# A hybrid retention and attention block: the row factor leaves the rotation of retention's keys and queries, and the setup is put in another order

## The chip, the cores and the metric

The kernel runs on one core of one Trainium2 chip. The metric is the device time of one execution in microseconds (us), the median over runs of the kernel. Engine names in the profile: PE is TensorE (matrix products), PEld its weight loads, DVE is VectorE, ACT is ScalarE, POOL is GpSimd, SP is SyncE, which issues most DMA transfers here.

## What is computed

One layer over T = 16 + 1024 rows of width 1024 (16 learned meta rows are put in front). All of it is float32. The reference, cut:

```python
u = _rms_norm(h, pre_w)                      # h * rsqrt(mean(h*h) + eps) * pre_w
rq, rk, rv, rg, aq, ak, av, ag, gr, ga = _split_in(u @ w_in)
rq = _pad_front(_rotary(rq.reshape(B, T, RET_HEADS, RET_DK), pos))
rk = _pad_front(_rotary(rk.reshape(B, T, RET_HEADS, RET_DK), pos) * (RET_DK ** -0.5))
o_r = _bidirectional_retention(rq, rk, rv, lg_f, lg_b)[:, META_PAD:]
o_r = (o_r - mu) * lax.rsqrt(var + EPS)      # per row and head, over 256 values
y_r = (o_r * ret_nw * silu(rg)) @ w_rb
y_a = (_windowed_sink_attention(aq, ak, av, sink) * silu(ag)) @ w_ab
out = (sigmoid(gr) * y_r + sigmoid(ga) * y_a) @ w_o
return h + _rms_norm(out, post_w)
```

Retention, for a chunk of 128 rows and one direction, is `inner = (q kT * decay) v`, `cross = (q * q_decay) S` and the state `S = chunk_decay * S + (k * k_decay)T v`. There are four heads, with 128 columns of q and k and 256 of v.

The normalization of a row is one number, r = (mean(x*x) + eps) to the power -1/2. Every projection of u is r times the projection of x * pre_w, so r can be put in late. In retention a key and its value always meet in a product, and a query stands alone in its output row: with unscaled keys and queries, v * r * r gives each key row its two factors, and the output row takes the query's r.

## The kernel before

*Products.* A float32 product is made of three fp32r products: each operand is split into a high part (hi, rounded) and the rest (lo), and `mm3` adds hi·hi, lo·hi, hi·lo (lines 70, 71 and 72 of the profile). ScalarE or GpSimd writes a hi, VectorE a lo (`dve_lo`, L78). Weights come as two raw tiles `wr` a unit and are split into `wh`, `wl` (`load_w`). The normalized input without its row factor, xT * pre_w, lies in SBUF as eight 128-row blocks (k = 0 to 7) of hi and lo, the tiles `big` (`xh[k]`, `xl[k]`).

*Setup.* For each k, ScalarE makes `xh` (L250), VectorE `xl` (L251), TensorE adds the block's part to all of head 0's q and k (`qk0_mm`, 18 products, into six PSUM banks `pq0`, `pk0`), ScalarE squares the raw block (L256). The squares are summed over k in two running sums (L260): blocks 0 to 4 on VectorE, the others (from `SQ2` = 5) on GpSimd. Then TensorE sums both over the partitions with a column of ones (L267, `pms`, plain float32), VectorE makes `ms` and GpSimd `rcol`, the row factor r with rows on partitions (L270, a power). The last block's `qk0_mm` comes after that in the text. `pv0` is the value projection of chunk 0 for head 0. `rw` and `rb` spread r over columns with TensorE, `rbc` is r along the free axis, and the rotation tables `cr` and `sr` are multiplied by it (L285, L286). After that `evac_qk0` rotates head 0's q and k out of PSUM (`rope_evac`: three VectorE products `m_qk`, L137 to L139, and one GpSimd sum, L140).

*Decays.* `decays()` makes lg, the log of the decay, from `dect` in a chain of some twenty 128x8 steps on GpSimd (L163 to L174), then `ex` (L176, L178) and with one power `dtab` (L181), the columns of decay factors. `decay_table` makes the 128x128 tables `DT` from lg: two VectorE products `dd` (L188, L189), an exponential on ScalarE, a scale on VectorE (L191).

*Retention.* For head h, `retention(h, fill)` runs `stage1(c + 1)` and `stage2(c)` over nine chunks (chunk 0 is the 16 meta rows), then a backward sweep. `stage1` makes pv (24 products; `pj`, three PSUM banks), its scaled parts `vh` (L373) and `vl` (L374), the transposed keys and the scores (`tr`, L377 and L379, bank `p1`), the decayed keys `khf`, `klf`, `khb`, `klb` (L387, L388) and the masked scores `sd`, `sh`, `sl`. `stage2` makes the outputs `pa`, evicted into `op` with `qdf` (L417, L418), and the states `pkv`, `Sf`, with their parts `Shf` (GpSimd) and `Slf`. `fill` runs a piece of the next head's q and k projections (`gen_qk`) in the backward sweep, and in the last head the first of attention's (`gen_ak`, `gen_aq`, `gen_gate`). Attention, gates and the three output products follow.

*Order.* Engines run their instructions in order. That order is not the text's: a scheduler with a time model orders the instructions of each engine when the kernel is built, so an instruction can stand well ahead of where the text has it. PSUM has eight banks: `pj` 3, `p1` 2, `p2` 2, `p3` 1; the six of the setup take two `pj`, one `p1`, both `p2` and `p3`.

## Time and profile before

| what | us |
|---|---|
| median of 3 runs | 1106.45 (1105.11 to 1109.32) |
| the profiled execution's own time | 1105.68 |
| its span, first to last instruction | 1103.9 |
| TensorE's granted clock over the span, share of full speed | 0.991 |

A row of the timeline or of a group reads: start, duration, engine, line, operation, output<-inputs with their shapes, count, and in brackets the idle time of that engine before it and what ended it. A row of waits reads: who waited, for whom, us in total, times, longest. A row of stretches reads: start:end and length in us, busy time (and instructions) of TensorE, its weight loads, VectorE, ScalarE and GpSimd, then TensorE's mean granted clock as a share of full speed, the share of the DMA engines in use and GB/s. Durations of instructions that follow one another closely overlap a little, so from start to start is what an instruction costs in a row of others.

### The profile page before, as it was taken

The page shows a single profiled execution, that of the slowest core. Times are in us where ns is not written, and L with a number is a line of the kernel's source. Part 1 is how long each engine was busy: PE and PEld are TensorE (multiplying, and loading weights), DVE is VectorE, ACT ScalarE, POOL GpSimd, SP SyncE. Part 2 cuts the span into 40 slices and gives each one's busy share as a digit, 9 for nine tenths or more (in the row PEclk, how much of TensorE's full clock was granted, in tenths as well). Part 3 has the DMA queues.
Part 4 walks back from the last instruction along what each step waited for, and adds up shares of the span by engine and source line. Part 5 has one row for each costly group of instructions (what it writes and reads, how often), then busy time and mean ns, then how long its engine had stood idle before and what let it go on. Part 6 is the DMA issues. An engine that isn't in the chain of part 4 may idle for free.

```text
span 1103.9 us, 17325 instructions
## 1 busy us (share of the span) xinstructions
PE 1077.2 (98%) x6034; PEld 929.5 (84%) x6034; DVE 863.3 (78%) x1830; ACT 486.8 (44%) x1126; POOL 255.9 (23%) x378
## 2 busy tenths in 40 slices
PE   6899999999999999999999999999999999999996
PEld 5799999999988888988888787888888788787885
DVE  5477787878976798988667876888889889867765
ACT  6132141422513544545557644445456546433442
POOL 7532433323232245455220000000000000010032
PEclk9799999999999999999999999999999999999998
DMA  7201111102114971021114753779783765789463
GB/s 285 77 1 39 58 58 39 52 26 66 52 48 134 346 245 58 21 96 39 68 48 153 257 200 109 231 242 357 264 274 125 233 205 192 236 202 332 116 115 76
DMA packets 75655, 159.45 MB, mean 144 GB/s; under 512 B 7984, under 2 KB 19760, under 8 KB 74800
## 3 DMA queue, kind: packets, MB, share of 16 engines
q1 hardware_dynamic: 72112, 152.06, 40.4%
q0 software_dynamic: 3456, 6.29, 3.9%
q8 instruction: 47, 0.77, 0.3%
q14 instruction: 40, 0.33, 0.1%
HBM read 105.89 MB, written 52.43 MB: 143 GB/s over the span
## 4 chain that ended last, share of the span: by engine, by line
PE 88%; DMA 4%; POOL 3%; ACT 2%; DVE 2%; issue 1%; SPq 1%; DVEq 0%; POOLq 0%; ACTq 0%
PE bz L70 7%; PE bz L71 6%; PE bz L72 6%; PE pv L70 3%; PE pv L72 3%; PE pv L71 3%; PE paq L71 3%; PE paq L72 3%; PE paq L70 3%; PE bo L71 2%; PE br L71 2%; PE bo L70 2%; PE bo L72 2%; PE br L70 2%; PE br L72 2%; PE ba L71 2%
## 5 line engine op out<-in xcount | busy, mean ns | idle before, releaser
L940 POOL DMA_DIRECT2D mx_d<-c1a x4 | 3.7, 920 | 398.1 <-DVE c1a L931 398.1
L71 PE MATMUL bz<-big,llz 128*128 128x512 f32 x208 | 82.5, 397 | 0.4 <-DVE llz L78 0.3
L71 PE MATMUL pv<-wh,big 128*128 128x256 f32 (+1 forms) x288 | 82.4, 286 | 0.0
L70 PE MATMUL pv<-wh,big 128*128 128x256 f32 (+1 forms) x288 | 81.8, 284 | 0.2 <-DVE vl L374 0.2
L72 PE MATMUL bz<-big,lhz 128*128 128x512 f32 x208 | 81.9, 394 | 0.0
L72 PE MATMUL pv<-wl,big 128*128 128x256 f32 (+1 forms) x288 | 81.6, 283 | 0.0
L70 PE MATMUL bz<-big,lhz 128*128 128x512 f32 x208 | 81.4, 396 | 0.2 <-ACT lhz L661 0.2
L70 PE MATMUL bz<-T,lhz 128*128 128x512 f32 x156 | 61.7, 396 | 1.7 <-ACT T L638 1.3
L71 PE MATMUL bz<-T,llz 128*128 128x512 f32 x156 | 61.5, 394 | 0.0
L78 DVE TENSOR_TENSOR wl<-wr,wh 128x1024 fp32r<-128x1024 f32 x34 | 46.4, 1365 | 19.3 <-POOL wh L75 19.2
L72 PE MATMUL bz<-T,lhz 128*128 128x512 f32 x156 | 61.3, 394 | 0.0
L1091 ACT ACTIVATE p<-p,nm 128x400 f32<-128x400 f32 (+1 forms) x64 | 38.3, 600 | 35.6 <-DVE nm L1089 32.8
L70 PEld LDWEIGHTS pv<-wh,big 128*128 128x128 f32 (+1 forms) x288 | 51.4, 179 | 1.7 <-DVE vl L374 0.9
L1102 POOL TENSOR_SCALAR p<-p,den 128x400 f32<-128x400 f32 (+1 forms) x60 | 36.1, 612 | 71.9 <-DVE den L1097 42.4
L71 PEld LDWEIGHTS pv<-wh,big 128*128 128x128 f32 (+1 forms) x288 | 51.4, 178 | 1.2
L72 PEld LDWEIGHTS pv<-wl,big 128*128 128x128 f32 (+1 forms) x288 | 51.4, 179 | 0.9
L71 PE MATMUL paq<-big,wl 128*128 128x512 f32 x128 | 51.3, 401 | 0.0
L70 PE MATMUL paq<-big,wh 128*128 128x512 f32 x128 | 51.0, 399 | 0.0
L72 PE MATMUL paq<-big,wh 128*128 128x512 f32 x128 | 50.9, 397 | 0.0
L70 PEld LDWEIGHTS bz<-big,lhz 128*128 128x128 f32 x208 | 39.1, 188 | 10.2 <-ACT lhz L661 1.1
L71 PEld LDWEIGHTS bz<-big,llz 128*128 128x128 f32 x208 | 39.1, 188 | 9.8 <-DVE llz L78 0.9
L72 PEld LDWEIGHTS bz<-big,lhz 128*128 128x128 f32 x208 | 39.1, 188 | 8.8
(593 smaller groups left out, 3636.0 us busy)
## 6 DMA issues: line engine op xcount, KB each, us to landing
wr<-in_w_in_dram SPq DMA_DIRECT2D x35, 512.0 KB, 3.6
wrz<-in_w_in_dram SPq DMA_DIRECT2D x28, 512.0 KB, 5.3
tg<-tg_d SPq DMA_DIRECT2D x32, 256.0 KB, 4.4
T<-preT SPq DMA_DIRECT2D x6, 1024.0 KB, 7.7
oTr_d<-ost SPq DMA_DIRECT2D x16, 256.0 KB, 2.1
xs<-in_xT_dram SPq DMA_DIRECT2D x16, 256.0 KB, 5.1
xsT<-xs SPq DMA_DIRECT2D x16, 256.0 KB, 5.1
oTa_d<-oa SPq DMA_DIRECT2D x16, 256.0 KB, 2.2
```

What stands on the lines that cost most here:

```text
L70: nc.tensor.matmul(o, ah, bh, start=first, stop=False, **kw)
L71: nc.tensor.matmul(o, al, bh, start=False, stop=False, **kw)
L72: nc.tensor.matmul(o, ah, bl, start=False, stop=last, **kw)
L78: nc.vector.tensor_tensor(o, i, hi.bitcast(F32), ALU.subtract)
L940: nc.gpsimd.dma_start(d, to, accum_op=ALU.add)
L1091: nc.scalar.activation(p[:, 0:wid], p[:, 0:wid], AF.Exp, scale=-1.0, bias=nm_[:, e_:e_ + 1], accum_out=den[:, e_:e_ + 1])
L1102: nc.gpsimd.tensor_scalar(pt[e_][:, 0:wid], pt[e_][:, 0:wid], den[:, e_:e_ + 1], 1.0, op0=ALU.mult, op1=ALU.mult)
```

## The change

- Head 0's q and k, and those of every head, are rotated with the plain tables. Values are scaled by `r2` = 1 / ms, which is r * r, in place of r. The output takes r of its row: the eviction of `pa` on ScalarE is scaled by `rcol`, and the factors on the cross terms are `qd` = rcol * dtab, eight small VectorE products for all heads and chunks.
- `rbc` and the tables with r are made later: `row_factors()` runs at the start of the last head, since attention and the gates still use them. The spreading products become transposes.
- All squares are summed on VectorE, in a chain (`q_ = sq + q_`). The sum is split into `sqh` (ScalarE) and `sql` (VectorE), and TensorE sums the two with fp32r ones, two columns wide.
- All eight blocks of `qk0_mm` run in the loop; the first piece of `evac_qk0` stands ahead of the sum, the others behind it. `pv0` of its own is gone.
- `ex` is made on ScalarE and in `decay_columns`; `dtab` is scaled on VectorE. `decay_table` for head h + 1 is called in head h.
- `tc.issue_after(split)` puts every instruction that its block traces on the engine of `split` (VectorE, the one that makes `sql`) behind it in that engine's order; other engines get no such edge.
- Loads: x block 0's first half and `dect` go to ScalarE's queue, ahead of and behind its first activation; `tabt` goes behind the rotation tables; `xr` has eight buffers in place of six.

In the built order of the changed kernel, VectorE's `dd` and `DT` stand behind `sql`; on ScalarE the product `ex` = lg * 128 stands right ahead of `xh` of block 5; VectorE's rotations of all six pieces of head 0 stand ahead of the first `vl`; TensorE's order behind the last `qk0_mm` is pv of chunk 0, of chunk 1, the sums `pms` (one of them inside pv of chunk 0), pv of chunk 2, transposes and the first `pkv`, then pv of chunk 3.

The diff, cut to its core:

```diff
-    def dve_lo(o, i, hi):
-        nc.vector.tensor_tensor(o, i, hi.bitcast(F32), ALU.subtract)
+        return nc.vector.tensor_tensor(o, i, hi.bitcast(F32), ALU.subtract).ins
...
-            g.tensor_scalar(ex[:, 4 * j:4 * j + 4], lg[:, base:base + 4], idx[:, j:j + 1], 1.0, op0=ALU.mult,
-                            op1=ALU.mult)
-        g.tensor_scalar(ex[:, 20:28], lg, float(P), 1.0, op0=ALU.mult, op1=ALU.mult)
-
-    def decay_columns():
+            nc.scalar.activation(ex[:, 4 * j:4 * j + 4], lg[:, base:base + 4], AF.Copy, scale=idx[:, j:j + 1])
+        nc.scalar.activation(ex[:, 20:28], lg, AF.Copy, scale=float(P))
         nc.gpsimd.tensor_tensor(dtab, ecst, ex, ALU.pow)
         for a, b in ((0, 8), (16, 20)):
-            nc.gpsimd.tensor_scalar(dtab[:, a:b], dtab[:, a:b], SCALE, 1.0, op0=ALU.mult, op1=ALU.mult)
+            nc.vector.tensor_scalar(dtab[:, a:b], dtab[:, a:b], SCALE, None, op0=ALU.mult)
...
-        nc.sync.dma_start(dect, dec.partition_broadcast(P))
-        xr = [st.tile([P, T], F32, tag="xr", bufs=6, name=f"xr{k}") for k in range(KT)]
+        xr = [st.tile([P, T], F32, tag="xr", bufs=KT, name=f"xr{k}") for k in range(KT)]
...
+        nc.scalar.dma_start(xr[0][:, 0:528], xT[0, :, 0:528])
+        nc.scalar.dma_start(dect, dec.partition_broadcast(P))
+        nc.sync.dma_start(vec, vecs)
...
-            if k < KT - 1:
-                qk0_mm(k)
-            q_ = st.tile([P, T], F32, tag="sq" if k else "sq0", bufs=4 if k else 1, name=f"sq{k}")
+            qk0_mm(k)
+            q_ = st.tile([P, T], F32, tag="sq", bufs=4, name=f"sq{k}")
             nc.scalar.activation(q_, t, AF.Square)
-            if k in (0, SQ2):
-                sq.append(q_)
-            else:
-                (nc.gpsimd if k > SQ2 else nc.vector).tensor_tensor(sq[-1], sq[-1], q_, ALU.add)
-        decay_columns()
-
+            if sq is not None:
+                nc.vector.tensor_tensor(q_, sq, q_, ALU.add)
+            sq = q_
+        wv0 = load_w(w_in, U_V, act=True)
+        evac_qk0(0)
+        sqh, sql = (st.tile([P, T], R, name=n) for n in ("sqh", "sql"))
+        nc.scalar.copy(sqh, sq)
+        split = dve_lo(sql, sq, sqh)
         pms = p1("pms")
         for c in range(9):
             a, b = cols(c)
-            for i in range(2):
-                nc.tensor.matmul(pms[0:b - a, c:c + 1], sq[i][:, a:b], ones, start=i == 0, stop=i == 1)
+            for i, t in enumerate((sqh, sql)):
+                summed = nc.tensor.matmul(pms[0:b - a, 2 * c:2 * c + 2], t[:, a:b], ones, start=i == 0, stop=i == 1).ins
...
+    nc.vector.reciprocal(r2, ms)
+    with tc.issue_after(split):
+        decay_columns()
     nc.gpsimd.tensor_tensor(rcol, ms, mhalf[:, 0:9], ALU.pow)
-    qk0_mm(KT - 1)
     nc.vector.tensor_copy(ident, tabt[:, 0:P])
-    wv0 = load_w(w_in, U_V, act=True)
-    pv0[0] = projT(wv0, 0, "pv0_0")
...
+    with tc.issue_after(split):
+        decay_table((0,))
+    for j in range(2 * NH):
+        nc.vector.tensor_scalar(qd[:, j], rcol[:, 1:9], dtab[:, 8 + j:9 + j], None, op0=ALU.mult)
...
-            nc.scalar.activation(vh[0:n], pv[0:n, 0:256], AF.Copy, scale=rcol[0:n, c:c + 1])
+            nc.scalar.activation(vh[0:n], pv[0:n, 0:256], AF.Copy, scale=r2[0:n, c:c + 1])
...
-                nc.scalar.copy(o, pa[:, 0:256])
-                nc.vector.scalar_tensor_tensor(o, pa[:, 256:512], qdf(h), o, op0=ALU.mult, op1=ALU.add)
+                nc.scalar.activation(o, pa[:, 0:256], AF.Copy, scale=rcol[:, c:c + 1])
+                nc.vector.scalar_tensor_tensor(o, pa[:, 256:512], qdf(h, c), o, op0=ALU.mult, op1=ALU.add)
...
-        if h == 0:
-            decay_table((1, 2, 3))
...
+            if c == 4 and h < NH - 1:
+                decay_table((h + 1,))
...
-    evac_qk0()
+    with tc.issue_after(split):
+        evac_qk0(1, 2, 3, 4, 5)
     for h in range(NH):
+        if h == NH - 1:
+            row_factors()
         fill, drain = filler([*([gen_qk(h + 1)] if h < 3 else [gen_ak(0), gen_aq(0, 0), gen_gate(7)])])
-        retention(h, fill)
-        drain()
+        with tc.issue_after(split):
+            retention(h, fill)
+            drain()
```

`row_factors()` holds the loop over `rw`, `rb`, `rbc`, `cr` and `sr` that stood in the setup, with `nc.tensor.transpose(t[...], rw[0:n], ident[0:n, 0:n])` for the product.

89 lines of the change are left out of this document (45 added, 44 removed).

## The prediction

> **What bounds the kernel now.** I read the page's first two parts, then TensorE's waits, then the stretches of the first 80 us, then the timeline there engine by engine. The page:
>
> ```profile
> span 1103.9 us, 17325 instructions
> PE 1077.2 (98%) x6034; PEld 929.5 (84%) x6034; DVE 863.3 (78%) x1830; ACT 486.8 (44%) x1126; POOL 255.9 (23%) x378
> PE   6899999999999999999999999999999999999996
> ```
>
> TensorE is busy for 98% of the span, so time can only be won where it idles or runs at a low clock. Its waits, total, times and longest:
>
> ```profile
> PE pq L70 <- ACT big L250: 6.8, 1, 6.8
> PE pms L267 <- POOL sq L260: 2.8, 1, 2.8
> PE pq L71 <- DVE w L78: 2.5, 1, 2.5
> ...
> PE to L457 <- ACT ost L462: 0.5, 1, 0.5
> ```
>
> The three long ones are all in the setup. In the four heads of retention the longest is 0.5 us, so what the change does to the heads' dependencies has almost nothing to win there. Stretches (start:end, length, busy time and count of each engine, granted clock, DMA):
>
> ```profile
> 20.50:30.00 9.50, 6.77 (x32) 5.65 (x31) 8.74 (x14) 6.84 (x9) 9.14 (x10) 0.82 0.42 149
> ...
> 36.50:46.20 9.70, 7.00 (x35) 6.99 (x35) 1.23 (x1) 0.00 (x0) 3.58 (x3) 0.64 0.23 76
> 46.20:52.00 5.80, 5.80 (x36) 4.66 (x37) 1.45 (x3) 1.10 (x5) 2.83 (x2) 0.72 0.07 12
> ...
> 60.00:70.00 10.00, 10.00 (x84) 9.73 (x82) 9.71 (x21) 1.20 (x3) 4.06 (x5) 1.00 0.01 2
> ```
>
> From 36.5 to 46.2 us TensorE only waits and sums squares, and each restart after idling runs at a low clock: 0.18 of 9.5 us and 0.28 of 5.8 us are 1.7 and 1.6 us lost. From 60 us on VectorE is full too (9.71 of 10), with TensorE still full: the pv projections cover it.
>
> Why it waits, from the timeline (start, length, engine, line, what):
>
> ```profile
> 6.65 1.66 POOL L165 TENSOR_TENSOR e<-e,neg 128x8 f32<-128x8 f32 x1
> 10.27 0.62 POOL L75 TENSOR_SCALAR w<-wr 128x512 fp32r<-128x512 f32 x1 [1.39 <-DMA wr<-in_w_in_dram]
> 10.44 1.54 DVE L251 SCALAR_TENSOR_TENSOR big<-xr,vec,big 128x1040 fp32r<-128x1040 f32 x1 [1.26 <-ACT big L250]
> 12.51 1.23 DVE L260 TENSOR_TENSOR sq<-sq,sq 128x1040 f32<-128x1040 f32 x1
> 12.72 1.08 POOL L170 TENSOR_TENSOR acc<-acc,ss 128x8 f32<-128x8 f32 x1
> 13.80 1.29 DVE L251 SCALAR_TENSOR_TENSOR big<-xr,vec,big 128x1040 fp32r<-128x1040 f32 x1
> 13.88 1.26 POOL L171 TENSOR_SCALAR acc<-acc 128x8 f32<-128x8 f32 x1
> 15.01 1.23 DVE L260 TENSOR_TENSOR sq<-sq,sq 128x1040 f32<-128x1040 f32 x1
> 16.17 1.29 DVE L251 SCALAR_TENSOR_TENSOR big<-xr,vec,big 128x1040 fp32r<-128x1040 f32 x1
> 17.60 0.20 POOL L170 TENSOR_TENSOR acc<-acc,ss 128x8 f32<-128x8 f32 x1
> 17.89 0.20 POOL L171 TENSOR_SCALAR acc<-acc 128x8 f32<-128x8 f32 x1
> 21.26 0.51 DVE L188 TENSOR_SCALAR dd<-tabt,lg 128x128 f32<-128x128 f32 x2 [3.80 <-POOL lg L174]
> ```
>
> The 128x8 steps of GpSimd's decay chain take 0.20 us, 0.29 from start to start, while VectorE idles, but while VectorE runs its 1040-wide operations each lasts until the running one ends (12.72+1.08 = 13.80, where the next starts): one step per VectorE operation. VectorE then waits 3.8 us for lg, the end of that chain, its split of the second weights comes late, and TensorE waits 2.5 us.
>
> **The change part by part.** Blocks k = 0 to 7 are the eight 128-row blocks of x; xh and xl are their parts (the tile big), V is the end of the first vl.
>
> *Start.* The first half of x block 0 goes to ScalarE's queue as its first instruction, and w's first part loses one issue before it:
>
> ```profile
> 2.11 0.43 SPq L216 DMA_DIRECT2D xr<-in_xT_dram  x1
> 5.92 1.35 ACT L250 ACTIVATE big<-xr,vec 128x528 fp32r<-128x528 f32 x2 [3.70 <-DMA xr<-in_xT_dram]
> ...
> 12.04 0.40 PE L70 MATMUL pq<-big,w 128*128 128x512 f32 x1
> ...
> 14.88 0.39 PE L70 MATMUL pq<-big,w 128*128 128x512 f32 x1
> ...
> 16.74 1.16 ACT L250 ACTIVATE big<-xr,vec 128x1040 fp32r<-128x1040 f32 x1
> ...
> 17.81 1.05 ACT L256 ACTIVATE sq<-xr 128x1040 f32<-128x1040 f32 x1
> ...
> 18.77 1.15 ACT L250 ACTIVATE big<-xr,vec 128x1040 fp32r<-128x1040 f32 x1
> ...
> 28.10 1.98 ACT L99 CAST wh<-wr 128x1024 fp32r<-128x1024 f32 x2
> ```
>
> Issue to use was 3.8 us; from 0.7 that is 4.5, and TensorE starts near 5.3 instead of 6.8. Its first block took 5.2 us (to 12.04), each later one 2.84.
>
> *VectorE no longer waits for lg; ScalarE does.* The order edge moves dd behind the split sql on VectorE. But ex = lg x 128 now stands on ScalarE, and in the changed kernel's built order it is the instruction ahead of xh of block 5, so xh5 is queued behind lg, and xl5, TensorE's block 5 and every later one wait for it. When is lg there? GpSimd ended the third w split at 10.9; now it begins its chain when dect, issued behind ScalarE's table load, is there, near 5.7 by my estimate, and with two pow of 1.66, two small w of 0.4, one step and w of 0.62 ends that split near 10.3, with 20 steps left. VectorE's xl1, at 10.44 before, hangs on x block 1, issued two places of 0.43 earlier: 9.6. From there it runs without a stop four xl of 1.21, four sq sums of 1.16 and two weight splits (0.62 and 1.14): 11.2 us, to 20.8, and ten steps pass. The other ten take 2.9 with VectorE idle: lg at 23.7, xh5 at 25.0 (0.2 and 1.15). TensorE wants block 5 at 5.3+5.2+4x2.84 = 21.9: a gap of 3.1 us takes the place of the old 2.5, with its cold restart. A restart lost 1.7 and 1.6 above, and 2.4 in the first block (5.2 less 2.84); I take 2.0. From 25.0, three blocks and a restart end the last at 35.5.
>
> *Squares.* Two sums of the tail leave GpSimd (its sums ended at 39.2) for VectorE, and one of the chain's heads becomes another sum: VectorE has seven at 1.16. The sum of squares becomes 18 fp32r products, 2 wide, for 36 fp32 pieces, 34 of them in the first row here:
>
> ```profile
> 39.20 7.12 PE L267 MATMUL pms<-ones,sq 128*16 128x1 f32 x34 [2.84 <-POOL sq L260]
> ...
> 59.31 0.28 PE L70 MATMUL pv<-wh,big 128*128 128x256 f32 x1
> 61.20 0.61 PE L283 MATMUL rb<-ident,rw 128*128 128x128 f32 x4
> 61.56 0.36 PE L71 MATMUL pv<-wh,big 128*128 128x256 f32 x1
> ```
>
> No row shows such a product: 0.09 (a 128x128 piece of rb, 0.36/4) and 0.21 (7.12/34) bound it, 1.6 to 3.8 us; I take 0.1, 1.9. They stand behind pv of chunks 0 and 1, so nothing is idle before them, and the next wait hides either price; uncovered they cost 1.9.
>
> *The new path: VectorE to the first vl.* Keys and queries rotate without the factor, so the built order puts all six rotations ahead of vl of chunk 0, and TensorE can take only pv 0 to 2 (three banks) before it. Rows:
>
> ```profile
> 31.28 1.21 DVE L78 TENSOR_TENSOR wl<-wr,wh 128x1024 fp32r<-128x1024 f32 x1
> 32.42 0.60 DVE L189 SCALAR_TENSOR_TENSOR dd<-tabt,lg,dd 128x128 f32<-128x128 f32 x2
> ...
> 64.83 0.41 DVE L137 TENSOR_TENSOR m_qk<-pk,cr 128x256 f32<-128x256 f32 x1
> ...
> 66.15 0.69 DVE L137 TENSOR_TENSOR m_qk<-pq,cr 128x512 f32<-128x512 f32 x1
> ...
> 68.28 0.34 DVE L388 SCALAR_TENSOR_TENSOR klf<-tr,dtab,khf 16x128 fp32r<-16x128 f32 x1
> ```
>
> From xh5 at 25.0: xl5 26.2; xl6 behind xh6 (two ScalarE operations of 1.01 later) 28.2; sq5, xl7, two small ones, sq6 32.0; wl 33.2; sq7 34.3; wl 35.5; rotation of the first k piece 36.9; sql 38.0. Then three k rotations of 1.32, two q rotations of 2.13, two wl of 1.14, nine dd and DT of about 0.25 (2.1), thirteen small ones (1.2) and klf and vl (0.27, 0.4): 14.5, V = 52.5. The small ones (qd, ms, reciprocal and the like) have no rows; at 0.06 to 0.2 each they would be 0.8 to 2.6. GpSimd's rotation sums, its two wh and rcol fit into that. A pv, 24 pieces 256 wide, is worth a block less 1%, 2.8. TensorE ends pv 2 at 35.5+3x2.8+1.9 = 45.8 and then waits some 6.5 us, a wait that was not there, with a restart of 2.0 behind it. Late with it are vh, kh and the pkv of all chunks, and pv 3, whose bank vl frees.
>
> The Trainium skill, SBUF — State Buffer, Who interferes with whom, says that GpSimd and a VectorE operation with two SBUF inputs exclude each other for a whole instruction, whichever came first. The trace agrees, the other way round too: the xl at 10.44 met GpSimd's w and took 1.54, not 1.29. By that rule the wl and dd between sql and V, which meet GpSimd's wh and rotation sums, would wait for them too; three such meetings at the 0.62 of that w would bring V 2 us later and the gain to 3.4.
>
> *Put at nothing.* The scaled eviction of op on ScalarE (44% busy) and qd for dtab: hidden behind TensorE. row_factors in head 3 puts six table products on VectorE, about 3 us, hidden behind the projections of a full TensorE; if that cover is gone, 3 us. Its nine transposes replace 18 pieces: 1.0 for 1.6. wr for V waits on the same splits as before and is there by 23.
>
> *The sum, equal work on TensorE.* Before, pv 3 starts at 59.3; three transposes, two score products, four pkv pieces (1.2) and the rb left (0.4) make it 60.9. After: 52.5, 0.1, 2.0 for the clock, 1.0 for the later transposes: 55.6. Gain 5.3. The profiled execution took 1105.7 (span 1103.9 and 1.8 around it), so 1100.4; the median of the runs, 1106.45, is 0.8 above it: I forecast 1101.
>
> **Rivals.** *lg is early.* If GpSimd gets several steps in between VectorE operations, xh5 follows at 20 and VectorE never stops: sql at 33.0 by the same list, V 5 us earlier, 1096. The lock step of 12.72 to 17.5 speaks against it; that any short wait of VectorE lets a step of 0.29 through, for it. *The gain is given back.* TensorE's order differs through heads and attention; if the waits there grow from about half a us per head to two, 5 us go, 1106. For it: VectorE 9.71 of 10. Against: heads 1 to 3 keep their order, seven pv ahead of the first pkv. *Slower:* in head 0 pv now leads pkv by three chunks, not seven. If VectorE, in its new order, serves each chunk's vl, kl, Sf and Slf one after another, the chain from pkv to the next pa (Sf, GpSimd's Shf and Slf, each about the 0.41 of a 256-wide m_qk, and the ways between; 2 us by estimate) stands bare for eight chunks: 16 us, 1117. It decides once a chunk's VectorE work (some seven such operations, 2.5 to 3 us, against 36 pieces at 2.8/24, 4.2, on TensorE) is stretched by half through waiting; for it speaks the in-order queue, against it that the rotations are done by then. *The change misses its aim* (squares and rotation as said, TensorE still waiting in the setup) is my forecast in part already: two gaps of 3 and 6.5 us remain.
>
> **How the numbers follow.** Forecast 0.5, own range 1097.5 to 1104.5; early lg 0.2; given back 0.19; slower 0.11. A measurement tells about 0.5% (5.5 us) from no change, so the edge is 1100.9, in the forecast's middle: faster 0.25+0.2 = 0.45; same 0.25+0.18 = 0.43; slower 0.12. The range takes in early lg with its spread below and the given-back case with the bounds above: 1092 to 1110.
>
> **What would show it.** TensorE waiting some 3 us for xh before block 5, behind ScalarE's ex on lg; no wait before pms, which is done near 43; a TensorE gap of about 6.5 us ending with the first vl near 52.5; no pause of VectorE between 28 and 52; heads' waits as before. It is wrong if lg comes by 21, if vl is not what ends the gap, or if the heads show new waits of several us.

## The result, and the profile after

The changed kernel takes 1112.87 us (median of 10 runs, 1111.64 to 1119.13) against 1106.99 (10 runs, 1105.11 to 1109.32): 1.0061 times as long, with a 95% interval of 1.0048 to 1.0075. It is slower, and outside the predicted range. Its profiled execution has a span of 1110.6 us and a mean granted clock of 0.985.

The page after, and then TensorE's waits:

```profile
span 1110.6 us, 17232 instructions
PE 1075.2 (97%) x6007; PEld 927.9 (84%) x6007; DVE 876.4 (79%) x1846; ACT 492.6 (44%) x1133; POOL 257.5 (23%) x368
```

```profile
PE pq L69 <- POOL w L74: 5.5, 1, 5.5
PE tr L388 <- DVE ms L284: 3.0, 1, 3.0
PE pq L69 <- ACT big L262: 3.0, 1, 3.0
PE pkv L71 <- DVE vl L385: 2.9, 1, 2.9
PE tr L388 <- DVE klf L399: 2.7, 1, 2.7
...
PE pkv L70 <- DVE klf L399: 1.2, 1, 1.2
```

The wait before `pms` is gone and the start is 1.3 us earlier, as meant. The wait for lg has a successor, the one for `big` (that is `xh` of block 5). The three rows that end with ms, vl and klf are one pause, broken by a few instructions: TensorE has nothing until VectorE brings what head 0's first chunk needs. The last row is not in the setup but in head 3. The stretches of the changed kernel (columns as before) show what the waits leave out, the clock:

```profile
20.50:30.00 9.50, 6.51 (x32) 5.61 (x31) 4.25 (x5) 4.91 (x6) 3.53 (x13) 0.82 0.31 123
...
46.20:52.00 5.80, 1.90 (x15) 1.52 (x14) 5.59 (x13) 0.87 (x3) 1.17 (x2) 0.82 0.38 137
52.00:60.00 8.00, 3.42 (x9) 2.08 (x9) 7.85 (x15) 2.23 (x7) 5.96 (x6) 0.50 0.09 34
60.00:70.00 10.00, 8.36 (x49) 8.14 (x50) 8.68 (x30) 3.45 (x10) 1.31 (x4) 0.65 0.00 0
273.50:280.00 6.50, 4.79 (x26) 3.15 (x24) 5.36 (x15) 3.70 (x13) 1.41 (x3) 0.89 0.12 42
280.00:285.40 5.40, 5.40 (x26) 5.18 (x26) 4.08 (x12) 2.59 (x8) 0.81 (x2) 0.50 0.00 0
```

The last two are the start of head 3; the same stretches of the kernel before:

```profile
273.50:280.00 6.50, 6.40 (x46) 5.38 (x45) 5.86 (x20) 3.52 (x11) 2.58 (x5) 1.00 0.13 43
280.00:285.40 5.40, 5.40 (x49) 5.40 (x48) 3.80 (x10) 2.95 (x9) 1.45 (x2) 1.00 0.15 50
```

TensorE is called busy for all of 280 to 285.4 us in both, but after the change it does 26 products at a clock of 0.50 where it did 49 at 1.00. Busy time alone hides this; count and clock show it.

To see where the time is lost over the whole span, two traces are laid beside each other at equal work: the columns of all matmul records up to a moment are summed (those of `pms` and `rb`, which differ, left out), and the lag is how much later than the kernel before the same sum is reached. The totals agree within 0.1%, so a lag is good to about 1 us. The changed kernel lags by 2.5 us at 100 us, the end of the disturbance in the setup; by nothing at 260 (it gains 2 us near 140 and 1 near 205, where the heads change); by 5.9 at 290, after the start of head 3; by 7.2 at 740; and by 5.8 at 1060. So there are two losses: the setup gives 2.5 back where 5.3 were to be won, and head 3 costs 6.

The timeline of the setup, several engines in order of time:

```profile
24.85 0.20 POOL L175 TENSOR_TENSOR lg<-lg,acc 128x8 f32<-128x8 f32 x1
25.09 0.21 ACT L180 ACTIVATE ex<-lg 128x8 f32<-128x8 f32 x1 [7.04 <-POOL lg L175]
...
26.40 0.79 PE L69 MATMUL pq<-big,w 128*128 128x512 f32 x1 [2.99 <-ACT big L262]
...
32.36 9.15 POOL L181 TENSOR_TENSOR dtab<-ecst,ex 128x28 f32<-128x28 f32 x1 [7.30 <-ACT ex L179]
35.63 1.22 DVE L77 TENSOR_TENSOR wl<-wr,wh 128x1024 fp32r<-128x1024 f32 x1
...
38.13 1.24 DVE L77 TENSOR_TENSOR sql<-sq,sqh 128x1040 fp32r<-128x1040 f32 x1
41.54 1.08 DVE L183 TENSOR_SCALAR dtab<-dtab 128x8 f32<-128x8 f32 x2 [2.17 <-POOL dtab L181]
42.54 0.80 DVE L188 TENSOR_SCALAR dd<-tabt,lg 128x128 f32<-128x128 f32 x1
...
44.91 1.76 DVE L77 TENSOR_TENSOR wl<-wr,wh 128x1024 fp32r<-128x1024 f32 x1
...
58.24 2.60 DVE L294 TENSOR_SCALAR qd<-rcol,dtab 128x8 f32<-128x8 f32 x8
...
61.12 0.86 DVE L385 SCALAR_TENSOR_TENSOR vl<-pv,r,vh 16x256 fp32r<-16x256 f32 x2
```

VectorE stands still for 2.17 us before two scalings of `dtab`, 128x8, for which GpSimd's power is late: it takes 9.15 us (5.66 in the kernel before), and it starts only 7.30 us after lg, because the five `ex` of L179 stand behind the last square on ScalarE. Behind the scalings in VectorE's queue are five rotations that were ready. Then many entries cost more than their price: 1.76 for a weight split of 1.14, 0.80 for a dd, 2.60 for eight qd. The first vl ends at about 61.6. The row of eight qd hides that only two of them are dear; here is the first of them by itself, with what GpSimd runs beside it:

```profile
58.09 1.36 POOL L139 TENSOR_TENSOR qr<-m_qk,m_qk 128x512 f32<-128x512 f32 x1 [1.47 <-DVE m_qk L138]
...
58.24 1.23 DVE L294 TENSOR_SCALAR qd<-rcol,dtab 128x8 f32<-128x8 f32 x1
```

It ends at 59.47, GpSimd's rotation sum at 59.45. The third qd (0.66) ends in the same way 0.03 us behind GpSimd's `qh`, and the other six take 0.22 each. All the dear entries between sql and vl are of this kind: the scaling, two dd, a DT and two qd each end 0.03 to 0.09 us behind a GpSimd operation that ran beside them, and the two wl of 1.76 end 1.08 us behind one. The rotations' products, which read PSUM, take their usual 0.42 to 0.44 beside the same operations (0.68 and 0.69 for the wide ones).

And the start of head 3:

```profile
275.43 0.56 DVE L312 TENSOR_TENSOR cr<-cr,rbc 128x272 f32<-128x272 f32 x1
...
278.80 0.41 DVE L313 TENSOR_TENSOR sr<-sr,rbc 128x256 f32<-128x256 f32 x1
...
279.20 0.59 DVE L399 SCALAR_TENSOR_TENSOR klf<-tr,dtab,khf 16x128 fp32r<-16x128 f32 x2
...
279.58 0.58 PE L70 MATMUL pkv<-vh,klf 16*128 16x256 f32 x1 [1.22 <-DVE klf L399]
```

Six table products of `row_factors` stand ahead of klf, and the first `pkv` of the head waits for klf.

### The profile page after: what moved, and what is told of

It is laid out like the page before. It is cut to its first block, busy times and chain, and to the rows that moved or that the text cites. A ratio compares the mean times of both kernels' runs of the same rounds, so it can differ in the third digit from the quotient of the medians.

```text
span 1110.6 us, 17232 instructions
## 1 busy us (share of the span) xinstructions
PE 1075.2 (97%) x6007; PEld 927.9 (84%) x6007; DVE 876.4 (79%) x1846; ACT 492.6 (44%) x1133; POOL 257.5 (23%) x368
## 4 chain that ended last, share of the span: by engine, by line
PE 87%; DVE 6%; POOL 3%; ACT 2%; DMA 1%; issue 1%; SPq 0%; POOLq 0%; DVEq 0%; ACTq 0%
PE bz L70 7%; PE bz L69 7%; PE bz L71 7%; PE pv L69 3%; PE pv L70 3%; PE pv L71 3%; PE bo L70 2%; PE br L70 2%; PE bo L69 2%; PE bo L71 2%; PE br L71 2%; PE br L69 2%; PE paq L70 2%; PE paq L71 2%; PE paq L69 2%; PE ba L70 2%
## 5 line engine op out<-in xcount | busy, mean ns | idle before, releaser
L77 DVE TENSOR_TENSOR wl<-wr,wh 128x1024 fp32r<-128x1024 f32 x34 | 48.7, 1433 | 7.6 <-POOL wh L74 7.3
L69 PEld LDWEIGHTS pv<-wh,big 128*128 128x128 f32 (+1 forms) x288 | 52.9, 184 | 2.0 <-DVE m_qk L138 0.8
L70 PEld LDWEIGHTS pv<-wh,big 128*128 128x128 f32 (+1 forms) x288 | 52.8, 183 | 1.1
L473 ACT ACTIVATE ost<-to,rnw 128x128 f32<-128x128 f32 x64 | 20.0, 364 | 65.4 <-PE to L468 57.1
L74 POOL TENSOR_SCALAR wh<-wr 128x1024 fp32r<-128x1024 f32 x32 | 39.0, 1219 | 36.9 <-PE pav L70 16.3
L69 PEld LDWEIGHTS bz<-big,lhz 128*128 128x128 f32 x208 | 39.1, 188 | 9.7 <-ACT lhz L676 0.6
```

Source lines behind the costliest of these rows:

```text
L69: nc.tensor.matmul(o, ah, bh, start=first, stop=False, **kw)
L70: nc.tensor.matmul(o, al, bh, start=False, stop=False, **kw)
L74: nc.gpsimd.tensor_scalar(o, i, 1.0, 1.0, op0=ALU.mult, op1=ALU.mult)
L77: return nc.vector.tensor_tensor(o, i, hi.bitcast(F32), ALU.subtract).ins
L473: nc.scalar.activation(ost[0][:, e_, w0:w0 + P], to[:, P * e_:P * e_ + P], AF.Copy, scale=rnw[:, 2 * h + e_:2 * h + e_ + 1])
```

## The experiments

Two theories were set against each other (letters in an expectation name the theories of that run). The first: both losses come from VectorE's in-order queue, where work that nobody needs yet, or that waits, stands ahead of what TensorE wants (in the setup the decay factors, in head 3 the tables). The second: each loss has one cause of another kind (ScalarE's `ex` on lg; the transposes of `row_factors` on TensorE; the order edges), and taking that away restores the forecast. All results, with the lag at equal work in us against the kernel before:

| kernel | median us | ratio to before, 95% | lag at 100 | 260 | 290 | 400 | 1060 |
|---|---|---|---|---|---|---|---|
| after | 1112.87 | 1.0061 (1.0048 to 1.0075) | 2.5 | -0.2 | 5.9 | 4.6 | 5.8 |
| e2 ex on GpSimd | 1111.92 | 1.0049 (1.0037 to 1.0061) | -0.3 | -2.9 | 2.3 | 1.0 | 3.9 |
| e5 scaling on GpSimd | 1111.74 | 1.0048 (1.0035 to 1.0060) | 0.4 | -2.2 | 3.6 | 2.3 | 7.1 |
| e13 no edges | 1108.00 | 1.0010 (1.0001 to 1.0020) | -2.0 | -4.9 | 1.0 | -0.3 | 0.6 |
| e16 no edge on tables | 1110.35 | 1.0031 (1.0019 to 1.0043) | -0.1 | -2.6 | 2.6 | 4.7 | 4.4 |
| e17 no edge on rotations | 1110.54 | 1.0033 (1.0023 to 1.0044) | 0.7 | -2.3 | 2.8 | 1.5 | 4.1 |
| e14 loads alone | 1106.41 | 1.0004 (0.9991 to 1.0017) | -1.4 | -1.5 | -1.4 | -2.8 | 0.0 |
| e3 decay factors on ScalarE | 1103.35 | 0.9974 (0.9963 to 0.9984) | -6.9 | -9.7 | -3.8 | -5.2 | -3.2 |
| e9 e3, qd on VectorE | 1105.15 | 0.9979 (0.9967 to 0.9990) | -7.0 | -9.7 | -4.6 | -5.8 | -2.0 |
| e1 factors in mid head 3 | 1111.27 | 1.0042 (1.0030 to 1.0054) | 1.4 | -1.1 | -1.0 | 4.5 | 4.6 |
| e6 factors early | 1110.61 | 1.0033 (1.0021 to 1.0046) | 1.2 | 0.4 | 1.4 | 0.6 | 4.4 |
| e10 e3 and e6 | 1101.25 | 0.9939 (0.9925 to 0.9953) | -6.7 | -7.6 | -6.6 | -7.6 | -5.5 |
| e4 lean list, e1 | 1098.98 | 0.9937 (0.9924 to 0.9950) | -12.7 | -13.8 | -13.0 | -8.1 | -7.7 |
| e7 lean list alone | 1099.75 | 0.9940 (0.9926 to 0.9953) | -12.2 | -13.4 | -8.1 | -7.4 | -8.2 |
| e8 lean list, e6 | 1100.67 | 0.9948 (0.9936 to 0.9960) | -13.2 | -12.4 | -12.0 | -9.5 | -7.5 |
| e11 e10, late weights | 1097.45 | 0.9909 (0.9896 to 0.9922) | -10.8 | -11.5 | -10.5 | -11.8 | -9.6 |
| e12 e10, late tables | 1097.12 | 0.9905 (0.9890 to 0.9920) | -11.0 | -11.8 | -10.5 | -11.3 | -9.0 |
| e15 lean list, factors in head 2 | 1096.10 | 0.9899 (0.9882 to 0.9917) | -12.5 | -10.9 | -9.9 | -10.5 | -11.8 |

**The setup: ex, scaling and edges.** e2 takes `ex` back to GpSimd:

```diff
-            nc.scalar.activation(ex[:, 4 * j:4 * j + 4], lg[:, base:base + 4], AF.Copy, scale=idx[:, j:j + 1])
-        nc.scalar.activation(ex[:, 20:28], lg, AF.Copy, scale=float(P))
+            nc.gpsimd.tensor_scalar(ex[:, 4 * j:4 * j + 4], lg[:, base:base + 4], idx[:, j:j + 1], 1.0, op0=ALU.mult,
+                                    op1=ALU.mult)
+        nc.gpsimd.tensor_scalar(ex[:, 20:28], lg, float(P), 1.0, op0=ALU.mult, op1=ALU.mult)
```

> Edit: ex = lg x columns back on GpSimd, as in the kernel before; all else as changed. Both theories: the 3.0 us gap before block 5 is gone and xh5 ends near 22.5. Theory A: V, the end of the first vl (61.98 in the changed kernel), moves by less than 2 us, since GpSimd's chain now goes on in lock step while VectorE is busy, its pow still starts at 32 or later, still takes about 9 us, and VectorE still waits for it ahead of the dtab scaling; time 1111 to 1113, ratio 1.004 to 1.006. Rival B: the whole list moves up by the gap, V near 58 to 59, time 1108 to 1110, ratio 1.001 to 1.003.

The gap before block 5 is gone and the same work is reached some 6 us earlier than after the change at 30 us, but only 2.8 earlier at 100. The timeline of e2 says why:

```profile
31.98 0.21 POOL L175 TENSOR_TENSOR lg<-lg,acc 128x8 f32<-128x8 f32 x1
...
34.74 4.81 POOL L182 TENSOR_TENSOR dtab<-ecst,ex 128x28 f32<-128x28 f32 x1
39.58 1.09 DVE L184 TENSOR_SCALAR dtab<-dtab 128x8 f32<-128x8 f32 x2 [5.77 <-POOL dtab L182]
```

With no pause of VectorE the chain on GpSimd goes on in lock step, and lg comes 7 us later. VectorE, now early, waits 5.77 us for the same scaling, and the first vl is only 2.0 earlier. The gap before block 5 is real but mostly covered by the path through dtab.

e5 moves only the scaling:

```diff
-            nc.vector.tensor_scalar(dtab[:, a:b], dtab[:, a:b], SCALE, None, op0=ALU.mult)
+            nc.gpsimd.tensor_scalar(dtab[:, a:b], dtab[:, a:b], SCALE, 1.0, op0=ALU.mult, op1=ALU.mult)
```

> Edit: the changed kernel with the two scalings of dtab back on GpSimd, as in the kernel before; all else as changed. It takes the wait for pow (2.17 us) and the two scalings (1.08) out of VectorE's list, and leaves pow, qd, wl and dd where they are. If the in-order wait on VectorE is what makes V late: V 2 to 4 us earlier than 61.98, time 1109 to 1111, ratio to the kernel before 1.002 to 1.005. If it is only that dtab is late, which klf needs in either case: no change, 1113, ratio 1.005 to 1.007.

It wins 2.1 us at 100, the length of the wait, but V, the end of the first vl, comes only 1.6 us earlier (60.0 for 61.6), short of the 2 to 4 expected; VectorE now waits 2.01 us, until 43.30, for GpSimd's wh, which the power holds up too. Behind 400 us the 2 us are lost again, and the median is 1.1 below that of the change, less than the intervals tell apart.

e13 takes all four order edges out, e16 those on the tables and on retention (the one on `decay_columns` stays), e17 the one on the rotations:

```diff
-    with tc.issue_after(split):
-        decay_columns()
+    decay_columns()
...
-    with tc.issue_after(split):
-        decay_table((0,))
+    decay_table((0,))
...
-    with tc.issue_after(split):
-        evac_qk0(1, 2, 3, 4, 5)
+    evac_qk0(1, 2, 3, 4, 5)
...
-        with tc.issue_after(split):
-            retention(h, fill)
-            drain()
+        retention(h, fill)
+        drain()
```

> Edit: the changed kernel without its four order edges behind sql. The built order then has dtab's scaling ahead of sql instead of behind it, and two of the dd ahead of the last square sums. Theory A (VectorE's in-order wait for GpSimd's pow is what the edges are placed around, the list itself is as long): the wait for pow stands before sql instead, pms moves behind it, V stays within 2 us of 61.98 and the time within 2 us of 1113, ratio 1.004 to 1.008. Rival (the edges themselves make V late, by holding back dd and dtab): V 3 us or more earlier, time 1108 to 1110.

> Edit: the changed kernel without the edges on the decay tables (head 0's table, and retention's list, tables of heads 1 to 3 with it); the edges on dtab and on the rotations stay. The built order then has two dd and two more dd between sq, wl, sq and wl, where the changed kernel has these four back to back, and dtab's scaling stays right behind sql. In the kernel without any edge pow took 4.81 us from 32.64 on, in the changed kernel 9.15 from 32.36 on. If it is the four instructions back to back that keep pow from starting, pow takes about 5 us here too, dtab is there by 38, VectorE's wait ahead of the scaling is gone, V is 2 to 4 us earlier, time 1108 to 1110, ratio 1.001 to 1.004. If pow's length is set by something else (its place behind ex, or the rotations), it stays near 9, the wait stays near 2 us or below by what the dd take, and the time is 1111 to 1113.

> Edit: the changed kernel without the edge on rotations 1 to 5 alone. The built order has rotation 1 ahead of sql and dtab's scaling behind it as before, and sq, wl, sq, wl stay back to back. Same theory: pow still takes about 9 us and ends near 41.5, rotation 1's 1.3 us fills most of VectorE's wait for it, V is 1 to 2 us earlier, time 1110 to 1112, ratio 1.003 to 1.006. If the edge on the rotations is what costs (they are behind in any case by the wait), 1108 to 1109 here and nothing in the other run.

All edges together cost 4.5 us at 100 and about 5 in the median; those on the tables and on retention 2.6, that on the rotations 1.8, and within the lag's accuracy the two add up. So of the two expectations for e13 it is the rival that came true in the time, against theory A; V came 2.3 us earlier, less than the 3 that the rival named. How the edges do it differs. The timelines of e16 and then e17 around the power:

```profile
32.30 4.81 POOL L181 TENSOR_TENSOR dtab<-ecst,ex 128x28 f32<-128x28 f32 x1 [7.30 <-ACT ex L179]
...
32.33 0.29 DVE L188 TENSOR_SCALAR dd<-tabt,lg 128x128 f32<-128x128 f32 x1
32.55 1.23 DVE L269 TENSOR_TENSOR sq<-sq,sq 128x1040 f32<-128x1040 f32 x1
...
41.78 1.07 DVE L183 TENSOR_SCALAR dtab<-dtab 128x8 f32<-128x8 f32 x2
...
59.77 1.25 DVE L384 SCALAR_TENSOR_TENSOR vl<-pv,r,vh 16x256 fp32r<-16x256 f32 x3
```

```profile
32.10 1.24 DVE L269 TENSOR_TENSOR sq<-sq,sq 128x1040 f32<-128x1040 f32 x1
32.26 9.16 POOL L181 TENSOR_TENSOR dtab<-ecst,ex 128x28 f32<-128x28 f32 x1 [7.30 <-ACT ex L179]
...
35.54 1.22 DVE L77 TENSOR_TENSOR wl<-wr,wh 128x1024 fp32r<-128x1024 f32 x1
37.28 0.44 DVE L136 TENSOR_TENSOR m_qk<-pk,cr 128x272 f32<-128x272 f32 x1 [0.52 <-PE pk L71]
...
41.46 1.08 DVE L183 TENSOR_SCALAR dtab<-dtab 128x8 f32<-128x8 f32 x2 [0.24 <-POOL dtab L181]
```

In e16 a dd stands on VectorE where the power begins, and the power takes 4.81 us, as in e2 (VectorE waiting) and in e13 (a dd there too). In e17, as in the change, four 1024- or 1040-wide operations with two SBUF inputs (sq, wl, sq, wl) follow one another there, and it takes 9.16. That its length hangs on what VectorE does when it begins is shown by these runs. That it is shut out until the fourth has ended is argued: in e17 the power ends at 41.4, 4.81 before that is 36.6, and the last wl ends near 36.7. One row speaks against it: in the kernel before, the power began at 25.98 beside a two-input sum of squares, two two-input operations (xl, L251) followed without a pause, and it took 5.66 us. So the edge on the tables made the power late (4.81 without it, 9.15 with it), but how, by taking the one-input dd away from beside it or otherwise, is not shown; the edge on the rotations put the scaling, which waits for the power, ahead of work that was ready: in e17 two rotations stand before it, and 0.24 us of the wait of 2.17 are left.

e14 is the kernel before with nothing but the new loads of the first half of x block 0 and dect:

```diff
-        nc.sync.dma_start(vec, vecs)
-        nc.sync.dma_start(dect, dec.partition_broadcast(P))
...
+        nc.scalar.dma_start(xr[0][:, 0:528], xT[0, :, 0:528])
+        nc.scalar.dma_start(dect, dec.partition_broadcast(P))
+        nc.sync.dma_start(vec, vecs)
...
-        nc.sync.dma_start(xr[0][:, 0:528], xT[0, :, 0:528])
```

> Edit: the kernel before with the early start alone: the first half of x block 0 and the decays on ScalarE's queue, as in the change; all else as before. TensorE starts near 5.3 instead of 6.8. If the start's 1.5 us carry through: 1.5 us below the kernel before, ratio 0.9985. If the wait of VectorE's dd for lg, which GpSimd's lock step sets, takes them back: no change, ratio 0.9995 to 1.0005. The built order moves other instructions too (ident and the sums of squares), so a miss by 2 us would not be about the start.

The earlier start is carried as 1.4 us through head 3 and is given back in attention; the median doesn't move.

**The decay factors off VectorE and GpSimd.** e3 makes dtab with ScalarE's exponential behind the split of the squares, and scales it and makes qd there too; e9 is e3 with qd on VectorE as in the change.

```diff
-            nc.scalar.activation(ex[:, 4 * j:4 * j + 4], lg[:, base:base + 4], AF.Copy, scale=idx[:, j:j + 1])
-        nc.scalar.activation(ex[:, 20:28], lg, AF.Copy, scale=float(P))
-        nc.gpsimd.tensor_tensor(dtab, ecst, ex, ALU.pow)
+            nc.scalar.activation(dtab[:, 4 * j:4 * j + 4], lg[:, base:base + 4], AF.Exp, scale=idx[:, j:j + 1])
+        nc.scalar.activation(dtab[:, 20:28], lg, AF.Exp, scale=float(P))
...
-            nc.vector.tensor_scalar(dtab[:, a:b], dtab[:, a:b], SCALE, None, op0=ALU.mult)
+            nc.scalar.activation(dtab[:, a:b], dtab[:, a:b], AF.Copy, scale=SCALE)
...
-        nc.scalar.copy(sqh, sq)
+        squares = nc.scalar.copy(sqh, sq).ins
...
-    with tc.issue_after(split):
+    with tc.issue_after(split), tc.issue_after(squares):
...
-        nc.vector.tensor_scalar(qd[:, j], rcol[:, 1:9], dtab[:, 8 + j:9 + j], None, op0=ALU.mult)
+        nc.scalar.activation(qd[:, j], rcol[:, 1:9], AF.Copy, scale=dtab[:, 8 + j:9 + j])
```

> Edit: the decay columns dtab by ScalarE's Exp behind sqh (no ex, no GpSimd pow), their scaling and the eight qd on ScalarE too; the rest as changed, row factors in head 3 included. It takes from VectorE's list the 2.17 us wait for pow, two scalings of 0.54 and eight qd of 0.33, together 5.9 us, and the gap before block 5. Theory A: V near 53 to 56 and the time 5 to 7 us below the changed kernel's, 1106 to 1108, ratio 0.999 to 1.002. Rival B: as for ex on GpSimd, V 58 to 59, 1108 to 1110.

> Edit: the decay columns by ScalarE's Exp behind sqh, scaling on ScalarE, but the eight qd on VectorE as in the changed kernel (the experiment before had them on ScalarE). The first vl then stands behind them again. If the qd's 2.60 us in the changed kernel are the price of eight such instructions in that place, V is 2.5 to 3 us later than 52.7, and the time 2 to 3 us above 1103.4: 1105 to 1107, ratio 0.999 to 1.001. If they were stretched by what GpSimd did beside them, they take under 1.5 us here and the time is 1104 to 1105.

e3 is the first version faster than the kernel before; it lies 2.7 us below the range that theory A expected. At 100 us it leads the change by 9.4. The timeline of VectorE in e3, with one row of GpSimd:

```profile
32.64 1.24 DVE L77 TENSOR_TENSOR sql<-sq,sqh 128x1040 fp32r<-128x1040 f32 x1
...
36.81 1.78 DVE L77 TENSOR_TENSOR wl<-wr,wh 128x1024 fp32r<-128x1024 f32 x1
...
50.06 1.35 POOL L139 TENSOR_TENSOR qr<-m_qk,m_qk 128x512 f32<-128x512 f32 x1 [1.47 <-DVE m_qk L138]
50.21 1.35 DVE L188 SCALAR_TENSOR_TENSOR dd<-tabt,lg,dd 128x128 f32<-128x128 f32 x1
...
52.19 0.47 DVE L384 SCALAR_TENSOR_TENSOR vl<-pv,r,vh 16x256 fp32r<-16x256 f32 x1
```

No wait is left in its list, yet from the end of sql (33.9) to the first vl (52.7) it takes 18.8 us, where the prediction had 14.5 for more entries. So the list is longer than its prices by itself, beside the wait. Of the 8.9 us by which V leads that of the change, 5.5 come ahead of sql (33.9 for 39.4), where the pause before block 5 is gone, and 3.4 behind it (18.8 for 22.2). e9 answers neither way of its expectation: the eight qd are there again and take 2.59 us, but the first vl is only 0.5 later and the lag is the same. The rows say why. In e3 a dd of 0.34 stands beside GpSimd's last rotation sum (50.06 to 51.41) and takes 1.35; in e9 the first qd stands beside the same sum (49.68 to 51.04) and takes 1.23, and that dd, behind it, takes 0.34. So the price is that of GpSimd's sum and is paid by whichever entry meets it. A split of q (0.6) also stands behind the vl in e9.

**Head 3.** e1 calls `row_factors` at chunk 4 of head 3; e6 makes `rbc` in chunk 4 of head 1 and multiplies the tables (`scale_tables`, the second loop of `row_factors`) where head 2 ends:

```diff
+            if c == 4 and h == 1:
+                row_factors()
...
         if h == NH - 1:
-            row_factors()
+            scale_tables()
```

(e1: `h == NH - 1` in the first hunk, and no call in the second.)

> Edit: the changed kernel with the row factors (nine transposes, six table products) traced in the middle of head 3's forward loop, at chunk 4, instead of ahead of its first chunk. Theory A (two separate losses: VectorE's stretched list in head 0 costs the setup's gain; the six table products of 3.1 us, standing ahead of klf at the start of head 3, leave TensorE idle for 1.7 us and then at a clock of 0.50 for 5.4 us): about 4.5 us faster than the changed kernel, 1108 to 1109, ratio to the kernel before 1.001 to 1.003, no clock below 0.9 between 262 and 300 us. Rival B (the late xh of block 5, behind ScalarE's ex, is the one cause; what head 3 loses is only that delay taken in another place): no change, 1113, ratio 1.005 to 1.007.

> Edit: the changed kernel with the nine transposes and the three copies into rbc traced in head 1 (chunk 4, TensorE full), and only the six table products left ahead of head 3, where the built order puts them beside head 2's last rotations, well ahead of klf of head 3; TensorE's order in head 3 is then that of the kernel before, word for word. If head 3's loss (1.7 us idle, and 5.4 us at a clock of 0.50) comes from the factors standing at the foot of head 2's work: 4 to 5 us faster than the changed kernel, 1108 to 1109, ratio 1.001 to 1.003, clock 1.00 from 250 to 400. If the products cost VectorE the same wherever they stand, as the experiment at chunk 4 of head 3 could be read (only 1.6 us won): 1111 to 1113, ratio 1.004 to 1.006.

> Edit: decay columns and qd on ScalarE, as in the third experiment, and the row factors early (transposes and rbc in head 1, table products beside head 2's last rotations); head 3's order on TensorE is that of the kernel before. Theory that the two losses are separate, and that the lean list with early factors came to nothing only because three pb products stand without cover at the end of its head 3: 4 to 5 us below the third experiment, 1098 to 1100, ratio 0.992 to 0.995, no idle time over 1 us between 250 and 360. Theory that head 3's loss comes back in some later wait whatever is done: 1102 to 1104, ratio 0.996 to 0.998.

In e1 the step at 280 us is gone, but it is back at 350 to 360; the stretches of e1 there:

```profile
350.00:355.00 5.00, 3.61 (x30) 3.19 (x28) 3.52 (x12) 1.88 (x6) 0.76 (x2) 1.00 0.23 78
355.00:360.00 5.00, 3.06 (x10) 2.02 (x11) 3.37 (x14) 2.69 (x9) 1.74 (x5) 0.56 0.21 69
```

The projections that fill the backward sweep had been used up earlier (the last at 352.2), and the last two of its pb are left with nothing beside them. The loss had moved, not gone, and the time is 2 us above the expected. In e6 the stretches of head 3's start are nearly those of the kernel before:

```profile
273.50:280.00 6.50, 6.01 (x38) 4.50 (x37) 5.56 (x21) 3.77 (x12) 2.12 (x4) 1.00 0.25 82
280.00:285.40 5.40, 5.40 (x49) 5.40 (x48) 4.32 (x12) 2.75 (x9) 1.77 (x3) 1.00 0.02 7
```

and the step is 1.0 us, not 6.1. e10, which joins e3's diff and e6's, has the same step of 1.0 and keeps most of both gains, though both end above the expected time (1110.61 for 1108 to 1109, 1101.25 for 1098 to 1100). In e6 itself some 3 us are lost again behind 540 us, in attention and the gates; why is not settled.

**A leaner list.** In e4 and e7 the weight splits of head 1, and the decay tables of heads 1 to 3, stand behind the vl of chunk 4, on top of e3's diff; e7 leaves `row_factors` where the change has it, e4 puts it where e1 does, e8 where e6 does, e15 in chunk 5 of head 2. e11 is e10 with only the weights late, e12 with only the tables:

```diff
+            with tc.issue_after(edges["v"]), tc.issue_after(edges["q"]):
+                w = load_w(w_in, U_QK + h)
...
+            if h == 0 and c < 5:
+                edges["v"] = lo
...
-                decay_table((h + 1,))
+                with tc.issue_after(edges["v"]):
+                    decay_table((h + 1,))
```

> Edit: the lean list (decay columns and qd on ScalarE; head 1's weight splits and the decay tables of heads 1 to 3 behind vl of chunk 4) with the row factors where the changed kernel has them. V as in the lean list with the factors at chunk 4 (46.3), head 3 loses again what the changed kernel loses there, and the end of head 3's backward pass (340 to 350 us, 3.6 us idle) is full: 1098 to 1101, ratio 0.993 to 0.996. If the two places add up, the lean list alone is worth 1113 - 1099.5 = 13 us of the changed kernel's time; if head 3's loss only moves, it comes out level with the lean list before, 1099.

> Edit: all of the decay columns on ScalarE, and two more things off the list ahead of vl: the split of head 1's weights stands behind Sf of chunk 3 on GpSimd and vl of chunk 4 on VectorE, and the decay tables of heads 1 to 3 behind that vl too; and the row factors at chunk 4 of head 3. Theory A: two wl of 1.76 and six dd and DT of 0.3 to 0.4 less, about 5.6 us: V near 48 to 51; head 3 as in the experiment with the factors at chunk 4. Time 1097 to 1102, ratio 0.991 to 0.996. Rival B: the wl and dd only change places with idle time of VectorE, no more than 2 us beyond the decay columns and the gap: 1104 to 1108, ratio 0.998 to 1.001.

> Edit: the lean list and the row factors early (transposes and rbc in head 1, table products beside head 2's last rotations). If the setup's loss and head 3's are two separate ones, their mends add: 4 to 5 us below the lean list alone, 1094 to 1096, ratio 0.989 to 0.991. If head 3's loss moves on to the end of its backward pass, where three pb products stand without cover: 1098 to 1100, ratio 0.992 to 0.995.

> Edit: as decay columns on ScalarE with the row factors early, and head 1's weight splits behind Sf of chunk 3 and vl of chunk 4 of head 0; the decay tables stay. Two wl (1.78 and 1.21 us) leave VectorE's list ahead of vl: V 2.5 to 3 us earlier than in that experiment, and 2 to 3 us off the time: 1096 to 1098, ratio 0.990 to 0.993.

> Edit: as decay columns on ScalarE with the row factors early, and the decay tables of heads 1 to 3 behind vl of chunk 4 of head 0; the weight splits stay. Six dd and a DT (0.67, 0.6, 0.23, 0.79, 0.28, 1.35, 0.33 us) leave the list: V 3 to 4 us earlier than with the row factors early alone, and 2 to 3 us off the time: 1096 to 1098, ratio 0.990 to 0.993.

> Edit: the whole lean list (decay columns and qd on ScalarE, head 1's weight splits and the decay tables of heads 1 to 3 behind vl of chunk 4) with the row factors at chunk 5 of head 2, where the built order leaves two pb products without cover at the end of head 3, as in the kernel before, and not three. V near 46.3 as in the other lean lists; head 3 without the loss of 5 to 6 us at its start, and without the 4 us at its end that the lean list with early factors had: 1093 to 1096, ratio 0.987 to 0.990. If it comes out level with the two half lists (1097), the loss has found a third place.

The first vl comes at 45.1 to 46.1, and the lag at 100 goes from -6.9 to -12 or -13; either half of it is worth some 4 us (e11 and e12 against e10), both together 5 to 6.5. e7 then loses the 5.3 us of head 3's start, which shows that loss to be independent of the setup. e4 and e8 avoid it there and lose 3.9 and 2.6 between 340 and 400, where pb stand bare as in e1 (two in e4, one in e8). e15 takes the transposes into head 2 and has the lowest median: 1096.10 us, 0.9899 of the kernel before (0.9882 to 0.9917). The intervals do not tell it from e11 and e12. Beside e7 it loses 2.8 us between 100 and 260. Its trace shows a third place of the same kind: near the end of head 2 four of the table products (245.9 to 248.0) stand ahead of a vl, and TensorE waits 1.5 us for that vl. Its stretches:

```profile
46.20:52.00 5.80, 5.80 (x26) 5.20 (x25) 3.25 (x6) 2.35 (x12) 2.28 (x3) 0.52 0.00 0
...
273.50:280.00 6.50, 6.50 (x57) 6.50 (x56) 5.98 (x13) 2.36 (x7) 2.46 (x3) 1.00 0.34 124
```

Between 41 and 47 us TensorE still has only small products with pauses, and works at a clock of 0.52 until 52: half of 5.8 us by the clock, and the pauses beside it, are left in the setup even here.

## Why the prediction was wrong

*The start* was right: TensorE begins at 5.5 (5.3 forecast). So was *the gap before block 5*: 2.99 us behind `ex` on lg (3.1), at 26.4 for 25.0, since VectorE's first pause, in which the chain runs freely, began at 21.9 in place of 20.8. (The terms named for GpSimd's third w split add up to 10.7, not 10.3; the trace has 11.9, and nine steps of the chain passed in lock step in place of ten.)

*Squares* were right: 18 products at 0.11 us from start to start, done at 44.0 (43 forecast), and no wait before them.

*The new path, VectorE to the first vl* is the step that failed. It gave 52.5; the trace has 61.6. Of the 9.1 us, 1.4 are the later end of sql (39.4 for 38.0). 2.2 are the wait for dtab, against the sign it named, no pause of VectorE between 28 and 52: the prediction counted its scalings among "thirteen small ones" at 0.06 to 0.2 and never asked when their input is there, though it put `ex` behind lg, and the power needs `ex`; it looked at the order edge for what it moves (dd), not for what it puts behind a waiting instruction. The other 5.5 are entries dearer than their rows: eight qd 2.60 (0.7 in the sum), two scalings 1.08 (0.2), two wl 1.76 (1.14), two dd about 0.8 (0.25) and a DT 0.60. All of these are meetings with GpSimd, eight in number, and each entry ended with or behind GpSimd's operation; the sum took its prices from rows where no such operation stood beside them. The sentence on the Trainium skill (SBUF — State Buffer, Who interferes with whom), with V 2 us later through three meetings with GpSimd, pointed the right way and was left out of the sum; it had the price of a meeting nearly right (0.62; 5.5 us over eight are 0.69) and their number wrong, since a scaling, a DT and two qd, which it did not name, met GpSimd too. The forecast gain of 5.3 became a loss of 2.5, 7.8 us between them, for a V 9 us late. That the gap ends with vl was right: e2, e5, e13, e16 and e17 bring V forward by 0.9 to 2.3 us and win 1.8 to 4.5 at 100, so the time goes with V, though not one for one. It is not one gap, as forecast, but three, and the first two end with ms and klf, which stand in the same queue.

*row_factors put at nothing*: it named the cover, "the projections of a full TensorE", and 3 us if the cover is gone. The cover is not there, because in-order VectorE serves the tables before klf, for which head 3's first `pkv` waits. And 3 us was half the price: by estimate from the stretches, 1.6 more of idle time (6.40 less 4.79), 2.7 in the stretch at a clock of 0.50 (half of 5.4), 0.5 in the one at 0.89 (0.11 of 4.79), and about a us of transposes. Taken out (e6, e10), the step shrinks from 6.1 to 1.0.

*The rivals.* Early lg did not come about: lg was there at 25.05, 1.4 us later than in the forecast itself. Given back: true of small gains in attention (e14, e5), but not what made the change slow. The slower one was right in its sign and wrong in its place: from 70 to 125 us the lag stays between 2.4 and 3.4, so the chain from pkv to pa in head 0 costs nothing.

What stays open: why attention and the gates take 1 to 5 us more or less from one order of the same work to another (lags from 400 to 1060 us), and what holds the power for 9.15 us in some orders and lets it end after 4.81 or 5.66 in others.

## What to carry to other kernels

When an operation moves to another engine's in-order queue, ask of each new entry when its operands are there and what stands behind it; an order edge that puts a waiting instruction ahead of ready work costs the wait even where the instruction is tiny. Price each entry with what the other engines run beside it, too: here an entry of 0.22 us took 1.23 beside a GpSimd operation, and moving it away passed the price to its neighbour. "Hidden" has to be shown at the queue of the engine that does the work, against the next instruction that someone waits for, not by the busy share of the engine that is to cover it. A pause of TensorE can cost its length and then the time at the lower clock, which in head 3 was twice as much (1.6 us of idling, 3.2 by the clock).

## What the runs showed of the hardware

- A power of 128x28 on GpSimd took 4.81 us where VectorE waited or ran a one-input operation as it began (e2, e13, e16), 9.15 where four two-input operations stood in a row there (the change, e17), and 5.66 in the kernel before, where a two-input operation was running. The Trainium skill (SBUF — State Buffer, Who interferes with whom) has a VectorE instruction with two SBUF inputs and a GpSimd one that reads SBUF exclude each other for the whole instruction. The late start that the long power suggests agrees with that; what ran inside the power doesn't: in e16 an sq with two SBUF inputs ran inside it in its usual 1.23 us.
- GpSimd's 128x8 steps took 0.20 us alone and 1.05 to 1.28 beside 1040-wide operations of VectorE, through nearly the whole chain in e2.
- A 128x8 product on VectorE with a factor per partition (qd) took 0.22 us, 0.13 from start to start. Eight of them took 1.16 in e17, with no GpSimd operation beside them, and 2.6 in the change and in e1, e2, e5, e6, e9 and e16, where two of the eight took 1.23 and 0.66 and, in the change and in e9, ended 0.02 to 0.03 us behind a GpSimd operation.
- A 1024-wide weight split of 1.21 us on VectorE (two SBUF inputs) took 1.76 in the change where it met GpSimd's rotation sum, ending 1.08 us behind it.
- After pauses between few small products TensorE stayed at a clock of 0.50 for 5.4 us and more (280 to 285.4) although it was busy throughout.
